# Turning keys and values with VectorE and DRAM instead of TensorE, with the transfers on GpSimd's queue

## The chip, the cores and the metric

One core of a Trainium2 chip runs the whole program. The metric is device time in microseconds; three runs of the kernel before took 852.05, 852.40 and 853.03 us, median 852.4 us.

## The reference

A sequence of 512 tokens of width 1024 goes through two layers. Each layer does an RMS norm, one wide input projection, an attention mixer, a product with SiLU of a gate, an output projection and a residual add. All data is float32.

- Layer A has three dilated head groups of 16 heads of 64 each. Group 0 is a local window, groups 1 and 2 have dilations 4 and 16. Queries and keys are RMS-normed per head; the three groups' softmaxes are merged by their denominators, so one softmax over all three groups' logits gives the same result:

```python
for g, (window, dilation) in enumerate(DILATED_PAIRS):
    q = rms_norm(qkv[:, :, g, 0], q_gain[g])
    k = rms_norm(qkv[:, :, g, 1], k_gain[g])
    v = qkv[:, :, g, 2]
    o, lse = dilated_group_attention(q, k, v, ...)
alpha = jax.nn.softmax(jnp.stack(lses), axis=0)
y = jnp.sum(alpha[..., None] * jnp.stack(outs), axis=0)
y = y.reshape(b, s, BRANCH_WIDTH).astype(hn.dtype) * jax.nn.silu(gate)
return y @ w_out
```

- Layer B is a 2-D neighbourhood attention with one head group. The change does not touch it.

## The kernel before

**Tiling.** Heads are taken in eight pairs, `hc` = 0 to 7; a pair fills 128 partitions. For each pair of layer A `main_a` runs four projections: `rawk` (keys of groups 1 and 2 beside their values, 512 columns), `rawq` (queries of the three groups and keys of group 0, 512 columns), group 0's values (`v0_a`) and the gate (`gate_a`). Products are kept exact by splitting each operand into a rounded high part and a rest: `wh` is made by ScalarE (L127), `wl` by GpSimd for two splits of five and by VectorE for the others (L131), and each product is three matmuls (`mm3`). One split of 512 weight columns feeds twelve matmuls. There are four buffers each of `wh` and `wl`, and a split is made while the three before it are still to be used.

**Attention of a pair** (`attn_a`). `scores(u)` works on two of the four query tiles, `u` = 0 and 1: its logits come from `q0h`, `k0h` (group 0) and from `qt`, `k12` (groups 1 and 2). The exponentials `p` are turned by VectorE in blocks of 32x32 (`tr`, L727), then `turner.send` writes them to DRAM (`td`, L736) and four transfers read them back (`pt`, L740), which completes the transposition. `weigh` multiplies P^T with the values `v12` and `v0`; `put_y` applies the gate. Queries of pairs 0 to 5 (`moved`) take the same way through DRAM (`move_q`: `qd`, `qt`).

**Keys and group 0's values.** `k_a` turns the keys of groups 1 and 2 on TensorE: two groups of four 128x128 transposes (L210), each copied out of PSUM by VectorE with the gain `gk` (L527). `v_a` turns `vt` on TensorE with four transposes, and ScalarE copies them to `v0` (L615).

**Order.** TensorE's order is written out by hand: `run` steps through `main` (the projections) and lets `side` (attention) put its work between them, by a clock that counts TensorE's work in nanoseconds; a 512-column matmul counts 512/2.4 = 213. `later_on(delay, job)` emits a job when that clock has advanced by `delay`. The other engines' orders come from a planner, save where `keep_in_program_order` holds an instruction behind the one traced before it on its engine. Transfers of weights, `td`, `pt`, `qd`, `qt` and biases are all issued by SyncE.

Of the kernel before, what the change touches and what calls it, by code (L numbers as in the profile page):

```python
# [13 lines left out]
F32 = mybir.dt.float32  # L14
# [28 lines left out]
def tile_hybrid_encoder(  # L43
# [222 lines left out]
    def squares(v, ss, i, ns):  # L266
        sq = wk.tile([P, 512], F32, tag="sq", name="sq")[:, : ns * 64]
        if len(v.shape) == 3:
            v = v.rearrange("p (a f) r -> p a f r", f=4)
            nc.gpsimd.tensor_mul(sq.rearrange("p (f a r) -> p a f r", f=4, a=4), v, v)  # L270
        else:
# [7 lines left out]
    def head_norm(raw, ss, ns, held, delay=0):  # L279


        rs = wk.tile([P, 32], F32, tag="rs", name="rs")
        rsqrt(nc.vector if ns == 8 else nc.gpsimd, rs[:, : 4 * ns], ss[:, : 4 * ns], 4 * ns, 1.0 / DH)

        def scale():
            for i in range(4):
                by = rs[:, i * ns : (i + 1) * ns].unsqueeze(2)
                if len(raw.shape) == 4:
                    v = raw[:, :, i, :].rearrange("p (h a f) r -> p f h a r", h=2, f=4)
                    by = rs[:, i * ns : (i + 1) * ns].rearrange("p (f h) -> p f h", h=2)  # L290
                    by = by.unsqueeze(3).unsqueeze(4).to_broadcast([P, 4, 2, 2, 32])
                else:
# [34 lines left out]
    rs_n = cp.tile([P, 4], F32, name="rs_n")  # L327
    rs_trj = cp.tile([P, S], F32, name="rs_trj")
    rs_half = cp.tile([P, S], F32, name="rs_half")
# [40 lines left out]
    def scales_a():  # L370
        pa = spread()
        nc.scalar.mul(tjr(rs_half), to_tjr(pa), 0.5)
        nc.scalar.copy(trj(rs_trj), to_trj(pa))

# [49 lines left out]

    def part(n):
        return rk[:, 1024 * n : 1024 * n + 1024].rearrange("p (i c) -> p i c", i=4)

    def project_qk(n, ns, key, hc, guard, first=False, **kw):
# [3 lines left out]
        def evac(i, acc):  # L432
            if not box:
                if key == "rawq":
                    t = wk.tile([P, 4 * n], F32, tag="rawq", name=key, bufs=1)
                    box.append(
                        t.rearrange("p (c i r) -> p c i r", c=16, i=4)
                        if moved(hc)
                        else t.rearrange("p (i c) -> p i c", i=4)
                    )  # L440
                elif key == "rawk":
                    box.append(part(0))
                    st["v12", hc] = part(1 + hc % 3)
# [8 lines left out]
            elif key == "rawk":  # L452
                pieces = [(raw[:, i, :], acc[:, :256]), (st["v12", hc][:, i, :], acc[:, 256:])]
            else:
                pieces = [(raw[:, i, :], acc[:, :n])]
            for dst, src in pieces:
                if first:
                    nc.scalar.copy(dst, src)
                else:
                    nc.scalar.activation(dst, src, AF.Copy, scale=rs_n[:, i : i + 1])  # L460
            if not first:
                squares(raw[:, :, i, :] if key == "rawq" and moved(hc) else raw[:, i, : ns * 64], ss, i, ns)

# [8 lines left out]
    def normed(raw, ss, ns, key, hc):  # L472
        head_norm(raw, ss, ns, key == "raw", 9000 if key == "rawk" and 0 < hc < NHC - 1 else 0)
        if key == "rawq" and moved(hc):
            turn_q(raw)
        st[key, hc] = raw
        stamp[key, hc] = clock[0]

    def first_out():

        raw, ss = st.pop("first")
        for i in range(4):
            for t in (raw, st["v12", 0]):
                nc.scalar.activation(t[:, i, :], t[:, i, :], AF.Copy, scale=rs_n[:, i : i + 1])
            squares(raw[:, i, :], ss, i, 4)
        normed(raw, ss, 4, "rawk", 0)
# [12 lines left out]
    def v0_a(hc):  # L499
# [3 lines left out]
        vt = wk.tile([P, EXT], F32, tag="vt", name="vt", bufs=1)  # L503
        nc.vector.tensor_mul(trj(vt[:, 64:EXT]), to_trj(acc[0]), trj(rs_trj))
        nc.gpsimd.tensor_copy(vt[:, 0:64], vt[:, EXT - 64 : EXT])
        st["vt", hc] = vt
        stamp["vt", hc] = clock[0]
# [13 lines left out]
    def k_a(hc):  # L521
        yield "wait", ("rawk", hc), 12500 if hc == 0 else 22500 if hc < NHC - 1 else 10000
        k12 = wk.tile([P, 2, 512], F32, tag="k12", name="k12", bufs=1)
        raw = st.pop(("rawk", hc))
        for g in range(2):
            tp = transpose4(raw, g * P)
            nc.vector.tensor_scalar(k12[:, g, :], tp, gk[:, g + 1 : g + 2], None, op0=ALU.mult)  # L527
# [80 lines left out]
    def v_a(hc):  # L608
# [4 lines left out]
        for i in range(4):  # L613
            transpose(tp[:, i * P : (i + 1) * P], vt[:, i * P : (i + 1) * P])
        nc.scalar.copy(v0[hc % 2], tp.rearrange("p (i c) -> p i c", i=4))  # L615
        stamp["v", hc] = 0
# [99 lines left out]
    class turner:  # L716
# [11 lines left out]

        def send(self, dst, wait, pace):

# [4 lines left out]
            src = self.t[:, : 4 * run].rearrange("p (b x) -> p b x", b=4)  # L735
            tc.keep_in_program_order(nc.sync.dma_start(d.rearrange("b p x -> p b x"), src))  # L736

            def read(b):
                src = d[b].rearrange("(a k) x -> k a x", a=4)
                tc.keep_in_program_order(nc.sync.dma_start(place[32 * b : 32 * b + 32], src))  # L740
                self.left -= 1
# [4 lines left out]
    def attn_a(hc):  # L746
# [7 lines left out]
        def scores(u):  # L754
# [94 lines left out]
        if hc < NHC - 1:  # L849
            for u in range(2):  # L850
# [285 lines left out]
    def side():  # L1136
# [20 lines left out]
        for hc in range(NHC):  # L1157
            if hc < NHC - 1:
                yield from k_a(hc)
                yield from chain(q_a(hc), v_a(hc))  # L1160
                if moved(hc):
                    yield from st.pop(("land", hc))
                yield from attn_a(hc)
                if hc == 1:
# [113 lines left out]
```

## Time and profile before

| | |
|---|---|
| median of 3 runs | 852.4 us |
| the profiled execution's own time | 854.65 us |
| its span, first to last instruction | 852.7 us |
| TensorE matmul busy | 843.6 us, 99% |
| VectorE / ScalarE / GpSimd busy | 520.2 / 431.3 / 307.1 us |
| moved by DMA | 141.23 MB |

The profile names engines PE (matmul), PEld (weight load), DVE (VectorE), ACT (ScalarE), POOL (GpSimd) and SP (SyncE). A "q" behind a name is the engine's queue, where DMAs are issued. A timeline row gives start and duration in us, the engine, the line, what is written and read, and in brackets the engine's idle time before it with what ended it. A group row gives busy time in us and the mean of one in ns. Layer A takes roughly the first 550 us, layer B the rest.

### The profile page before, as it was taken

To read this page: it belongs to the slowest core of one execution; us is meant where nothing else is said; L and a number is where in the kernel's file an instruction comes from. 1 tells how busy PE (TensorE), PEld (TensorE's weight loads), DVE (VectorE), ACT (ScalarE), POOL (GpSimd) and SP (SyncE) were. 2 spreads that over 40 slices of the span, in tenths; PEclk is the share of its full clock that TensorE was granted. 3 is DMA by queue.
4 is the path that set the end of the run, shared out by engine and by line. 5 is a ranking of instruction groups with operands and counts; after the bars stand their busy time and mean duration, and the time that the engine had idled before them with its cause. 6 is when DMAs were issued, how large, how long until landed. Compare 5 with 4: busy or idle time off the path is not lost.

```text
span 852.7 us, 15400 instructions
## 1 busy us (share of the span) xinstructions
PE 843.6 (99%) x5547; PEld 702.7 (82%) x5547; DVE 520.2 (61%) x1335; ACT 431.3 (51%) x924; POOL 307.1 (36%) x493
## 2 busy tenths in 40 slices
PE   8999999999999999999999999999999999999998
PEld 6788878788788788788788787789998898889786
DVE  6445684674675675675675745447567656766642
ACT  7433653653652652652653554355366655665531
POOL 2252541542542542542531341121344335542411
PEclk9999999999999999999999999999999999999999
DMA  7346277477478378378375562174245654555223
GB/s 250 111 130 208 87 226 219 153 222 227 137 230 241 105 239 240 98 238 238 96 247 153 147 190 78 60 244 142 82 142 150 168 162 149 170 163 160 99 98 126
DMA packets 65372, 141.23 MB, mean 166 GB/s; under 512 B 5904, under 2 KB 23248, under 8 KB 65296
## 3 DMA queue, kind: packets, MB, share of 16 engines
q1 hardware_dynamic: 65008, 140.24, 53.7%
q8 instruction: 44, 0.72, 0.4%
q14 instruction: 32, 0.26, 0.1%
q10 hardware_dynamic: 288, 0.01, 0.0%
HBM read 109.11 MB, written 31.12 MB: 164 GB/s over the span
## 4 chain that ended last, share of the span: by engine, by line
PE 87%; ACT 4%; DMA 4%; DVE 3%; issue 1%; POOL 1%; SPq 0%; ACTq 0%; POOLq 0%; DVEq 0%
PE acc L206 74%; PE log L206 5%; PE o L206 5%; PE tp L210 3%; DMA qd<-rawq 1%; ACT p L655 1%; ACT p L814 1%; DMA rp<-in_rpb 1%; ACT p L1067 1%; DMA qt<-qd 1%; POOL sq L270 1%; ACT wh L127 1%; DMA hg<-in_head_gain 0%; DVE wl L131 0%; DMA eb<-lb_d 0%
## 5 line engine op out<-in xcount | busy, mean ns | idle before, releaser
L127 ACT CAST wh<-wraw 128x512 fp32r<-128x512 f32 (+1 forms) x276 | 162.0, 588 | 291.4 <-PE acc L206 251.0
L206 PE MATMUL acc<-wh,hn_h 128*128 128x512 f32 (+1 forms) x768 | 294.2, 383 | 1.7 <-ACT wh L127 0.9
L206 PE MATMUL acc<-wh,hn_l 128*128 128x512 f32 (+1 forms) x768 | 286.3, 373 | 0.0
L206 PE MATMUL acc<-wl,hn_h 128*128 128x512 f32 (+1 forms) x768 | 285.8, 372 | 0.4 <-DVE wl L131 0.4
L131 POOL TENSOR_TENSOR wl<-wraw,wh 128x512 fp32r<-128x512 f32 (+1 forms) x110 | 137.0, 1245 | 359.4 <-ACT wh L127 320.0
L131 DVE TENSOR_TENSOR wl<-wraw,wh 128x512 fp32r<-128x512 f32 (+1 forms) x166 | 111.1, 670 | 135.8 <-ACT wh L127 131.5
L206 PEld LDWEIGHTS acc<-wh,hn_h 128*128 128x128 f32 x768 | 144.6, 188 | 29.3 <-issue 4.9
L206 PEld LDWEIGHTS acc<-wh,hn_l 128*128 128x128 f32 x768 | 144.4, 188 | 20.8
L206 PEld LDWEIGHTS acc<-wl,hn_h 128*128 128x128 f32 x768 | 144.8, 189 | 19.8 <-DVE wl L131 0.9
L206 PE MATMUL acc<-hn_h,wh 128*128 128x512 f32 x192 | 77.0, 401 | 0.9 <-ACT rawq L460 0.6
L206 PE MATMUL acc<-hn_h,wl 128*128 128x512 f32 x192 | 74.9, 390 | 0.0
L206 PE MATMUL acc<-hn_l,wh 128*128 128x512 f32 x192 | 74.8, 390 | 0.0
L655 ACT ACTIVATE p<-p,mn 128x512 f32<-128x512 f32 (+3 forms) x128 | 69.3, 586 | 0.0
L814 ACT ACTIVATE p<-p,mn 128x512 f32<-128x512 f32 (+1 forms) x64 | 44.8, 701 | 45.0 <-DVE mn L803 44.1
L273 DVE TENSOR_REDUCE ss<-sq 128x4 f32<-128x256 f32 (+1 forms) x96 | 48.4, 504 | 30.7 <-POOL sq L272 19.7
L727 DVE STREAM_TRANSPOSE tr<-p 128x512 f32<-128x512 f32 (+1 forms) x80 | 53.7, 682 | 9.9 <-ACT p L655 9.5
L272 POOL TENSOR_TENSOR sq<-rawk 128x256 f32<-128x256 f32 x64 | 40.5, 639 | 52.7 <-ACT rawk L460 44.9
L206 PE MATMUL acc<-y_h,wh 128*128 128x512 f32 x128 | 52.1, 407 | 0.0
L206 PE MATMUL acc<-y_h,wl 128*128 128x512 f32 x128 | 50.0, 391 | 0.0
L206 PE MATMUL acc<-y_l,wh 128*128 128x512 f32 x128 | 49.9, 390 | 0.0
L206 PEld LDWEIGHTS acc<-hn_h,wh 128*128 128x128 f32 x192 | 36.1, 188 | 10.8 <-ACT rawk L460 2.1
L206 PEld LDWEIGHTS acc<-hn_h,wl 128*128 128x128 f32 x192 | 36.0, 188 | 7.7
(138 smaller groups left out, 1087.0 us busy)
## 6 DMA issues: line engine op xcount, KB each, us to landing
wraw<-in_w SPq DMA_DIRECT2D x95, 512.0 KB
wraw<-in_w SPq DMA_DIRECT2D x38, 384.0 KB
td<-tr SPq DMA_DIRECT2D x14, 1024.0 KB
pt<-td SPq DMA_DIRECT2D x56, 256.0 KB
qd<-rawq SPq DMA_DIRECT2D x6, 1024.0 KB
qt<-qd SPq DMA_DIRECT2D x24, 256.0 KB
td<-tr SPq DMA_DIRECT2D x6, 896.0 KB
pt<-td SPq DMA_DIRECT2D x24, 224.0 KB
```

The lines of the kernel that those rows point to most:

```text
L127: nc.scalar.copy(h, raw)
L131: eng.tensor_sub(l, raw, h.bitcast(F32))
L206: nc.tensor.matmul(o, l, r, **kw)
L210: nc.tensor.transpose(o, i, ident)
L270: nc.gpsimd.tensor_mul(sq.rearrange("p (f a r) -> p a f r", f=4, a=4), v, v)
L272: nc.gpsimd.tensor_mul(sq, v, v)
L273: nc.vector.tensor_reduce(ss[:, i * ns : (i + 1) * ns], sq.rearrange("p (a b) -> p a b", b=64), axis=AX.X, op=ALU.add)
L655: nc.scalar.activation(pr, pr, AF.Copy, scale=mn[:, 3:4])
L727: nc.vector.transpose(dst, src[:, :n].rearrange("p (i b k) -> p i b k", b=4, k=32))
L814: nc.scalar.activation(row, row, AF.Exp, bias=mn[:, 1:2], scale=-1.0, accum_out=mn[:, 2:3])
L1067: nc.scalar.activation(pr[:, o : o + n], pr[:, o : o + n], AF.Exp, bias=mn[:, 0:1], scale=-1.0, accum_out=mn[:, 2:3])
```

## The change

- The keys of groups 1 and 2 of pairs 0 to 6 (`moved_k`) are written by the evacuation in a layout `rk_a` in which VectorE turns 32x32 blocks in place (two instructions a pair). `move_k` writes them to DRAM (`kd`) in one transfer and reads them back in four; ScalarE then applies the gain, with two instructions a pair.
- Group 0's values of pairs 0 to 5 are turned by VectorE into a free strip of the same buffer and ride with the next pair's keys; GpSimd copies them to `v0` with a factor of 2, because `vt` is now scaled with `rs_half`, and the tile `rs_trj` is gone.
- `k12` has another layout, so that the score matmuls read their moving operand in four runs of 32.
- All transfers of `kd`, and layer A's `td` and `pt` of pairs 0 to 6, are issued by GpSimd. The reads of P^T come 16000 clock units after the write with 900 between them, instead of 8500 and 1200.
- `k_a` stays for pair 7 alone, `v_a` for pairs 6 and 7.

```diff
+            if len(raw.shape) == 5:
+                for g in range(2):
+                    tc.keep_in_program_order(nc.vector.transpose(raw[:, :, g, :, :], raw[:, :, g, :, :]))
...
+    moved_k = lambda hc: hc < NHC - 1
...
+    rk_a = rk[:, :1536].rearrange("p (a y) -> p a y", a=4)
...
+        if key == "rawk" and moved_k(hc):
+            move_k(hc, 17500 if hc else 4000)
...
-        nc.vector.tensor_mul(trj(vt[:, 64:EXT]), to_trj(acc[0]), trj(rs_trj))
+        nc.vector.tensor_mul(
+            in_trj(vt[:, 64:EXT], "t r j"), in_trj(acc[0], "j t r"), in_trj(rs_half, "t j r")
+        )
         nc.gpsimd.tensor_copy(vt[:, 0:64], vt[:, EXT - 64 : EXT])
+        if moved(hc):
+            src = vt[:, :S].rearrange("p (i b x) -> p i b x", i=4, b=4)
+            dst = rk_a[:, :, 256:].rearrange("p b (i x) -> p i b x", i=4)
+            tc.keep_in_program_order(nc.vector.transpose(dst, src))
+            stamp["v", hc] = 0
+            return
...
+    def move_k(hc, delay):
+        n = 384 if hc else 256
+        d = dr.tile([4, P, 384], F32, name="kd", tag="kd", bufs=2)
+        box = []
+        def write():
+            tc.keep_in_program_order(nc.gpsimd.dma_start(d.rearrange("a p y -> p a y")[:, :, :n], rk_a[:, :, :n]))
+            stamp["k12", hc] = 0
+        def read(a):
+            if not box:
+                box.append(wk.tile([P, 4, 384], F32, tag="k12", name="k12", bufs=1))
+            dst = box[0][32 * a : 32 * a + 32, :, :n]
+            src = d[a].rearrange("(b k) y -> k b y", b=4)[:, :, :n]
+            tc.keep_in_program_order(nc.gpsimd.dma_start(dst, src))
+        def landed():
+            kv = box[0]
+            for g in range(2):
+                k = kv[:, :, P * g : P * g + P]
+                tc.keep_in_program_order(nc.scalar.activation(k, k, AF.Copy, scale=gk[:, g + 1 : g + 2]))
+            if hc:
+                src = kv[:, :, 256:].rearrange("p b (i x) -> p b i x", i=4)
+                dst = v0[(hc - 1) % 2].rearrange("p i (b x) -> p b i x", b=4)
+                tc.keep_in_program_order(nc.gpsimd.tensor_scalar(dst, src, 2.0, None, op0=ALU.mult))
+            st["k12", hc] = kv, st.pop(("v12", hc))
+        later_on(delay, write)
+        for n_, a in enumerate((0, 2, 1, 3)):
+            later_on(delay + 16500, partial(read, a))
+        later_on(delay + 29500, landed)
...
-        def send(self, dst, wait, pace):
+        def send(self, dst, wait, pace, by=nc.sync):
...
-                                k12[hs, g, P * j : P * j + P],
+                                sb(k12[hs], P * g + 32 * j, [[384, 4], [1, 32]]),
...
-                send = partial(turned.send, pq[:, 2048 * u : 2048 * u + 2048], 8500, 1200)
+                send = partial(turned.send, pq[:, 2048 * u : 2048 * u + 2048], 16000, 900, nc.gpsimd)
...
-                yield from k_a(hc)
-                yield from chain(q_a(hc), v_a(hc))
+                yield from q_a(hc)
                 if moved(hc):
                     yield from st.pop(("land", hc))
+                else:
+                    yield from v_a(hc)
```

More of the change, by code (lines that the diff above doesn't have):

```diff
@@ L270, in squares @@
             nc.gpsimd.tensor_mul(sq.rearrange("p (f a r) -> p a f r", f=4, a=4), v, v)
+        elif len(v.shape) == 4:
+            nc.gpsimd.tensor_mul(sq.rearrange("p (g a x) -> p a g x", g=2, a=4), v, v)
         else:
@@ L460, in evac @@
                     nc.scalar.activation(dst, src, AF.Copy, scale=rs_n[:, i : i + 1])
-            if not first:
-                squares(raw[:, :, i, :] if key == "rawq" and moved(hc) else raw[:, i, : ns * 64], ss, i, ns)
+            if first:
+                return
+            if key == "rawk" and moved_k(hc):
+                v = raw[:, :, :, i, :]
+            elif key == "rawq" and moved(hc):
+                v = raw[:, :, i, :]
+            else:
+                v = raw[:, i, : ns * 64]
+            squares(v, ss, i, ns)
         tile_of = lambda hn: lambda k, i: hn[:, k, P * i : P * (i + 1)]
@@ L475, in normed @@
             turn_q(raw)
+        if key == "rawk" and moved_k(hc):
+            move_k(hc, 17500 if hc else 4000)
         st[key, hc] = raw
@@ L521, in k_a @@
     def k_a(hc):
-        yield "wait", ("rawk", hc), 12500 if hc == 0 else 22500 if hc < NHC - 1 else 10000
-        k12 = wk.tile([P, 2, 512], F32, tag="k12", name="k12", bufs=1)
+        yield "wait", ("rawk", hc), 10000
+        k12 = wk.tile([P, 4, 384], F32, tag="k12", name="k12", bufs=1)
         raw = st.pop(("rawk", hc))
```

40 lines of the change are left out of this document (26 added, 14 removed).

## The prediction

> **What bounds the kernel now.** I read the profile's first page first, then TensorE's waits. From the page, two of the first lines:
>
> ```profile
> span 852.7 us, 15400 instructions
> PE 843.6 (99%) x5547; PEld 702.7 (82%) x5547; DVE 520.2 (61%) x1335; ACT 431.3 (51%) x924; POOL 307.1 (36%) x493
> ```
>
> Only 9.1 us of the span have no matmul. In the view of waits TensorE has six rows, each shorter in total than the first, under 5 us together:
>
> ```profile
> PE acc L206 <- ACT rawq L460: 1.4, 2, 0.8
> ```
>
> So TensorE's instructions themselves are the bound: what is taken off it comes off the time, if nothing new makes it wait. The busy total cannot price an instruction, as matmuls overlap; spacing in the timeline can. Here are TensorE's rows around one group of key transposes and one group of value transposes:
>
> ```profile
> 56.77 0.39 PE L206 MATMUL acc<-hn_h,wl 128*128 128x512 f32 x1
> 57.01 0.60 PE L210 MATMUL tp<-ident,rawk 128*128 128x128 f32 x4
> ...
> 58.60 0.39 PE L206 MATMUL acc<-hn_h,wl 128*128 128x512 f32 x1
> ...
> 60.66 0.39 PE L206 MATMUL acc<-hn_h,wh 128*128 128x512 f32 x1
> ...
> 61.79 0.39 PE L206 MATMUL acc<-hn_h,wl 128*128 128x512 f32 x1
> ...
> 74.71 0.39 PE L206 MATMUL acc<-wh,hn_l 128*128 128x512 f32 x1
> ...
> 76.54 0.39 PE L206 MATMUL acc<-wh,hn_l 128*128 128x512 f32 x1
> ```
>
> Undisturbed, five steps of the projection take 61.79 - 60.66 = 1.13 us, 0.227 each. From 56.77 to 58.60 are six projection steps and one group of four transposes: 1.83 us, of which the six steps are 1.36. **A group of four costs TensorE 0.47 us** (the 0.60 of its row overlaps its neighbours). The value group from 74.71 to 76.54, again six steps, costs 0.47 too.
>
> **What the change takes off TensorE.** In the view of the tile `tp`:
>
> ```profile
> L210 PE MATMUL tp<-ident,rawk x128: 270/272/273, 57.0 to 803.9; 128*128 128x128 f32 x128
> L210 PE MATMUL tp<-ident,vt x32: 270/272/274, 74.9 to 549.4; 128*128 128x128 f32 x32
> ```
>
> Of the 128 with `rawk`, 64 are layer A's keys, 8 a pair (layer B's raw tiles share the buffer's name). Seven pairs lose 2 groups each and six pairs a value group: 14 + 6 = 20 groups, 80 transposes. 20 x 0.47 = **9.4 us**. What else could be gained is bounded by TensorE's own waits, under 5 us, of which none is on the parts removed.
>
> The score matmuls stay in number, but read `k12` in runs of 32 instead of 128 (so does pair 7). The nearest rows are P^T's products, which already read runs of 32, and the scores as they are:
>
> ```profile
> L206 PE MATMUL o<-pt,rawk 128*64 128x128 f32 x320 | 22.4, 278 | 0.9 <-DMA eb<-lb_d 0.9
> L206 PE MATMUL log<-k,qt 64*32 64x128 f32 x1024 | 18.9, 274 | 0.0
> ```
>
> 278 against 274 ns for 128 columns: I cost the layout at nothing; the high end is a rival below.
>
> **What it adds to VectorE, ScalarE and GpSimd.** Groups by form:
>
> ```profile
> L535 DVE STREAM_TRANSPOSE rawq<-rawq 128x512 f32<-128x512 f32 x24 | 16.0, 688 | 0.0
> L527 DVE TENSOR_SCALAR k<-tp,gk 128x512 f32<-128x512 f32 x16 | 11.5, 720 | 0.8 <-PE tp L210 0.8
> L615 ACT COPY v<-tp 128x512 f32<-128x512 f32 x8 | 4.7, 585 | 5.9 <-PE tp L210 5.9
> ```
>
> VectorE: 20 transposes x 0.69 less 14 evacuations x 0.72 = +3.7 us over layer A. ScalarE: 14 gain passes x 0.59 (the copy's price) less 6 copies and the one of `rs_trj` = +4.1 us. GpSimd: six copies of `v0`, at most 1.32 each (its `wl` of that size, quoted below, has two inputs) = +7.9 us. None is on TensorE's path while these engines keep ahead of it. One period of a pair shows how much room there is; columns are the stretch, its length, and busy time of PE, PEld, DVE, ACT, POOL:
>
> ```profile
> 286.60:350.70 64.10, 64.10 (x454) 52.13 (x452) 41.18 (x100) 32.25 (x63) 24.62 (x36) 1.00 0.64 192
> ```
>
> VectorE and ScalarE gain under 1 us in each 64.1, beside 22.9 and 31.9 us idle; the granted clock is 1.00.
>
> **The moved transfers, the real risk.** GpSimd gets 15 transfers a pair: `td` twice, `pt` eight times, `kd` once, and its four reads. No row before shows GpSimd issuing one. On SyncE's queue such a transfer occupies the queue for (minimum/median/maximum ns)
>
> ```profile
> L740 SPq DMA_DIRECT2D pt<-td x80: 312/423/1553, 110.9 to 778.9; - x80
> L736 SPq DMA_DIRECT2D td<-tr x20: 377/382/1623, 105.1 to 765.0; - x20
> ```
>
> Call GpSimd's price of one c. The bounds by these rows are 0.31 and 1.62 us; I take the medians, 0.4, the same instruction. Behind a transfer GpSimd holds the next `wl`, and TensorE waits for that. How late may a `wl` be?
>
> ```profile
> L127 ACT CAST wh<-wraw 128x512 fp32r<-128x512 f32 x196 | 121.1, 619 | 217.0 <-PE acc L206 180.5 <-DMA wraw<-in_w 21.2 <-issue 8.8
> L131 POOL TENSOR_TENSOR wl<-wraw,wh 128x512 fp32r<-128x512 f32 x81 | 106.7, 1317 | 287.7 <-ACT wh L127 263.5 <-issue 9.3 <-DVE mn L1057 5.8
> ```
>
> The cast waits for TensorE (180.5 us) to free one of four buffers; three splits of 12 x 0.227 = 2.72 us are then still ahead. So 8.16 - 0.62 - 1.32 = **6.2 us of slack**. The tightest place is the end of `rawq` in each period, in GpSimd's and SyncE's timelines:
>
> ```profile
> 309.45 3.43 POOL L270 TENSOR_TENSOR sq<-rawq 128x512 f32<-128x512 f32 x3 [0.79 <-ACT rawq L460]
> 312.84 1.29 POOL L131 TENSOR_TENSOR wl<-wraw,wh 128x512 fp32r<-128x512 f32 x1
> 314.10 1.48 POOL L270 TENSOR_TENSOR sq<-rawq 128x512 f32<-128x512 f32 x1
> 316.96 0.63 POOL L505 COPY vt<-vt 128x64 f32<-128x64 f32 x1 [1.38 <-DVE vt L504]
> 319.37 1.28 POOL L131 TENSOR_TENSOR wl<-wraw,wh 128x512 fp32r<-128x512 f32 x1 [1.78 <-ACT wh L127]
> ```
>
> ```profile
> 296.12 0.38 SPq L736 DMA_DIRECT2D td<-tr  x1
> ...
> 310.47 0.38 SPq L736 DMA_DIRECT2D td<-tr  x1
> ```
>
> The program's clock runs 0.227/0.213 = 1.064 slower on the chip. The first P^T write stays at 296.1, so its four reads move to 296.1 + 17.0 = 313.1 to 316.0; the second write stays at 310.5. `rawk` of this period ends near 281.4 (the chain of waits has its `weigh` behind it at 281.75), so the keys' reads, 34000 later, come at 317.6. Nine transfers thus fall between 310.5 and the `wl` of 319.37, where GpSimd has 8.9 us less 2.4 + 1.3 + 1.5 + 0.6 = 3.1 us free. That `wl` is late by 9c - 3.1, and TensorE waits once 9c - 3.1 > 6.2: **from c = 1.03 us on**. At 0.4 the lateness is 0.5 us and costs nothing. On the same queue stand the squares, for whose sums VectorE waits, and the copy of `vt`, for which the new transpose of the values waits, with VectorE's own `wl` behind it; they have fewer transfers ahead of them (three and five), so they decide later than the `wl`.
>
> Do the new waits hold? From the chain of waits, one write of 1024 KB and four reads of 256 KB through DRAM:
>
> ```profile
> 201.33 10.40 DMA qd<-rawq
> ...
> 213.78 5.63 DMA qt<-qd
> 281.75 3.62 PE o L206 x48
> ```
>
> P^T's reads now come 17.0 us after their write and the keys' 17.6 us after theirs, against 10.4, so GpSimd need not stand waiting; the keys' reads have 13.8 us to land before ScalarE's gain passes (47000 units behind `rawk`, at 331.4), against 5.6. SyncE loses these waits altogether.
>
> Here one page speaks against the change: the Trainium skill, "SBUF — State Buffer", section "SBUF: two separate sides", says that a transfer issued by GpSimd has its descriptors written by GpSimd's own cores, which cannot write while VectorE runs an instruction that takes both ports, and gives about 0.62 us alone and 3.1 beside such an instruction. By the first figure as c, an estimate, the sum is mine; by the second, 18.6 us would be lost in every period. No run here shows it yet, and VectorE's work in that stretch has few plain copies, the case the page names.
>
> **The sum.** 852.7 - 9.4 = 843.3 us of span, to which the profiled execution adds 854.65 - 852.7 = 1.95. That execution was 2.25 us above the median of the runs; against the median, 852.4 - 9.4 = **843.0 us**, my forecast.
>
> **Rivals.**
>
> *GpSimd's issuing holds the `wl` (ends slower).* A GpSimd instruction of one shape does not always take the same time here:
>
> ```profile
> L505 POOL COPY vt<-vt x8: 237/631/731, 63.0 to 513.6; 128x64 f32<-128x64 f32 x8
> ```
>
> So GpSimd is held by something, up to threefold. A c of 0.42 x 731/237 = 1.3 us loses 9 x 1.3 - 9.3 = 2.4 us in each of the six periods (pairs 1 to 6) that have both the keys' and P^T's transfers: 14.4 us, **857 us**. It decides from 1.03, and gain and loss balance at 6(9c - 9.3) = 9.4, c = 1.21. At c = 1.12 it takes back half the gain: 847.7. At SyncE's maximum of 1.62 it would be 843 + 31.7 = 875. Against it: the medians are far below 1.03. The page named above would be the cause of such a hold; by its second figure the loss would be the larger one given there.
>
> *The strided keys slow the scores.* If the 1024 matmuls with the keys, 18.9 us busy, took twice as long, this would be 843 + 18.9 = 862 us. The row of 278 ns speaks against it.
>
> *The transfers disturb the weights.* The change moves 2 x 0.79 MB more a period on top of 192 GB/s x 64.1 us = 12.3 MB, and two queues now share the engines. ScalarE already waited 21.2 us for weights (the row above) without TensorE stopping. If each period of six gave back 1.3 us, 851 us, no change.
>
> **How the numbers follow.** The forecast has 0.64 (its own range 841 to 847: 2 us of TensorE's present waits gone too, and up to 4 us of small new ones). GpSimd's issuing has 0.24: 0.08 for c between 1.03 and 1.21, most of it still faster, 0.16 beyond. The strided keys have 0.04, the disturbed weights 0.08, mostly no change. A measurement of this kernel tells about 0.2%, 1.7 us. Faster: 0.64 + 0.06 = 0.70; same: 0.02 + 0.07 = 0.09; slower: 0.16 + 0.04 + 0.01 = 0.21. The range goes from 841 to 857, the rival at 1.3 us; it leaves out the worse half of that rival and the strided keys, under 2 in 10.
>
> **What would show it.** Right: 80 fewer `tp` matmuls, TensorE's waits still under some 8 us, the spacing of the `log` matmuls unchanged, GpSimd's transfers well under 1 us. Wrong: TensorE waiting for `wl` of GpSimd at the end of `rawq`, in each period; VectorE waiting for `vt`; scores stretched beyond 1.2 us for 64.

## The result, and the profile after

The changed kernel is slower. Four runs took 861.42, 862.03, 865.15 and 865.85 us, against a median of 852.22 us for the kernel before on the same chip; the ratio is 1.0125 (95% interval 1.0111 to 1.0138). Two further runs, of 875.27 us (granted clock 0.982) and of 2122.08 us, fall in the slow state and are left out of it. The forecast was 843.0 us, the range 841 to 857. The profiled execution of after is the one of 861.42 us, the fastest of the four, and the profiled one of before (854.65 us) lay 2.4 us above its median; so the two profiles show 6.9 us of the 11.4 us between the medians.

From the page of after (span, engines, DMA queues, and the engines' shares of the chain that ended last):

```profile
span 859.6 us, 15330 instructions
PE 842.8 (98%) x5467; PEld 698.8 (81%) x5467; DVE 530.2 (62%) x1341; ACT 434.7 (51%) x931; POOL 374.6 (44%) x604
...
q1 hardware_dynamic: 49552, 110.87, 43.0%
...
q0 software_dynamic: 11312, 39.85, 16.0%
...
PE 80%; DMA 7%; DVE 6%; ACT 3%; issue 1%; SPq 1%; POOL 0%; ACTq 0%; DVEq 0%; POOLq 0%
```

TensorE has 80 matmuls fewer (5547 to 5467), yet its busy time is almost the same and the span is 6.9 us longer. `q0` is GpSimd's DMA queue, new in this kernel. TensorE's waits in after (us in total, times, longest):

```profile
PE log L206 <- ACT q0h L695: 3.4, 5, 1.1
PE acc L206 <- ACT rawq L479: 1.9, 2, 1.1
PE log L206 <- DVE q0l L699: 1.5, 5, 0.3
PE tp L210 <- DVE rawq L301: 1.2, 1, 1.2
```

The new rows that recur are the first and the third (the fourth is a single wait): at the first scores of pairs 1 to 5 TensorE waits for the split queries and keys of group 0 (`q0h`, `q0l`). ScalarE makes these splits behind the arrival of `qt`, the queries' way through DRAM. That way is later by steps. From TensorE's side each stall starts a second loss; two stretches of after (length, busy time and instructions of PE, PEld, DVE, ACT, POOL, then the granted clock, the DMA share, GB/s):

```profile
286.60:350.70 64.10, 63.02 (x426) 51.21 (x426) 43.26 (x101) 32.39 (x63) 32.81 (x46) 0.97 0.71 208
290.40:293.80 3.40, 3.40 (x71) 2.69 (x72) 1.57 (x9) 1.39 (x2) 1.85 (x2) 0.50 0.02 5
```

After the stall at 288 us the granted clock is 0.50 for 3.4 us; the same happens once more at 161 us. Each dip loses 3.4 x 0.5 = 1.7 us. Reading the spacing of TensorE's instructions in the timeline, the stalls at the five first scores come to about 9.5 us, other new stalls to about 3, the dips to 3.4: 9.4 us saved, some 16 lost, which is the +6.9 of the span.

**Where the queries are late.** VectorE's timelines from the third sum of squares to the end of the queries' turn, before and then after:

```profile
312.91 0.69 DVE L273 TENSOR_REDUCE ss<-sq 128x8 f32<-128x512 f32 x1 [0.31 <-POOL sq L270]
...
320.96 2.50 DVE L295 TENSOR_TENSOR rawq<-rawq,rs 128x512 f32<-128x512 f32 x4
...
326.79 1.29 DVE L535 STREAM_TRANSPOSE rawq<-rawq 128x512 f32<-128x512 f32 x2
```

The same rows of after, with those between that are new there:

```profile
316.68 0.69 DVE L275 TENSOR_REDUCE ss<-sq 128x8 f32<-128x512 f32 x1 [0.31 <-POOL sq L270]
...
325.57 0.69 DVE L131 TENSOR_TENSOR wl<-wraw,wh 128x512 fp32r<-128x512 f32 x1 [1.13 <-ACT wh L127]
326.18 1.35 DVE L115 SCALAR_TENSOR_TENSOR na<-na,nv 128x32 f32<-128x32 f32 x1
327.46 0.68 DVE L523 TENSOR_TENSOR gt<-gt,rs_half 128x512 f32<-128x512 f32 x1
...
328.27 3.60 DVE L301 TENSOR_TENSOR rawq<-rawq,rs 128x512 f32<-128x512 f32 x4
...
332.46 2.48 DVE L608 STREAM_TRANSPOSE rawq<-rawq 128x512 f32<-128x512 f32 x4
```

From the sum to the end of the turn it was 328.08 - 312.91 = 15.2 us and is 334.94 - 316.68 = 18.3: a `wl` that waits for ScalarE and a step of the gate (`gt`) now stand ahead of the queries' scaling, and the scaling itself takes 3.6 us instead of 2.5. GpSimd's timeline of after shows a part of the cause:

```profile
317.84 0.79 POOL L809 DMA_DIRECT2D td<-tr  x1
318.63 0.56 POOL L813 DMA_DIRECT2D pt<-td  x1
319.20 1.05 POOL L270 TENSOR_TENSOR sq<-rawq 128x512 f32<-128x512 f32 x1
...
329.39 1.33 POOL L131 TENSOR_TENSOR wl<-wraw,wh 128x512 fp32r<-128x512 f32 x1 [1.91 <-ACT wh L127]
```

Two transfers, 1.35 us, now stand ahead of the fourth square of the queries. And a scaling is not slower as such: three of the four take 0.69 us, and the one that runs beside the `wl` of 329.39 takes 1.78. Of the 32 scalings in layer A, seven take about 1.78 us in after, and each of the seven starts while a `wl` of GpSimd is running; the other 25 take 0.68 to 0.69 us. Before, two are long.

Then the transfers, in SyncE's timelines before and after:

```profile
329.79 0.43 SPq L578 DMA_DIRECT2D qd<-rawq  x1
...
336.39 1.75 SPq L584 DMA_DIRECT2D qt<-qd  x4
```

and in after:

```profile
335.97 0.43 SPq L651 DMA_DIRECT2D qd<-rawq  x1
...
346.50 1.75 SPq L657 DMA_DIRECT2D qt<-qd  x4
```

Between the queries' write and their reads lay 6.6 us, and now 10.5. Not every pair is like this one, pair 4: in pairs 1 and 2 the time did not grow (9.1 and 10.5 us before, 7.3 and 9.9 in after), in pairs 3 to 5 it grew by 2.5 to 4.1. The slack shows at the other end. Before, the split `q0h` of this pair starts at 346.25 us, 4.8 us ahead of the first scores (351.00); in after it starts at 354.41, and the scores follow it directly, at 355.18. Why the write takes longer is seen in the queues of after from 336 to 340 us (packets, MB, share of the 16 DMA engines' time):

```profile
q0 software_dynamic: 272, 0.89, 98.9%
q1 hardware_dynamic: 16, 0.04, 4.4%
```

The queries' write was given to SyncE's queue at 335.97 and gets almost nothing for these four microseconds, while the reads on GpSimd's queue are being served. At the end of this way ScalarE, which the page before shows with no lack of time, stands still (timeline of after):

```profile
338.83 1.34 ACT L593 ACTIVATE k<-k,gk 128x512 f32<-128x512 f32 x2 [4.91 <-DMA k<-kd]
...
353.40 1.10 ACT L676 CAST k0h<-qt 128x512 fp32r<-128x512 f32 x1 [5.06 <-DMA qt<-qd]
```

### The profile page after: what moved, and what is told of

The parts are those of the page before. It is cut to its first block, busy times and chain, and to the rows that moved or that the text cites. A ratio compares the mean times of both kernels' runs of the same rounds, so it can differ in the third digit from the quotient of the medians.

```text
span 859.6 us, 15330 instructions
## 1 busy us (share of the span) xinstructions
PE 842.8 (98%) x5467; PEld 698.8 (81%) x5467; DVE 530.2 (62%) x1341; ACT 434.7 (51%) x931; POOL 374.6 (44%) x604
## 4 chain that ended last, share of the span: by engine, by line
PE 80%; DMA 7%; DVE 6%; ACT 3%; issue 1%; SPq 1%; POOL 0%; ACTq 0%; DVEq 0%; POOLq 0%
PE acc L206 70%; PE log L206 5%; DMA qt<-qd 3%; PE o L206 3%; DMA qd<-rawq 2%; PE tp L210 2%; DMA k<-kd 1%; DVE rawq L301 1%; ACT k0h L676 1%; SPq L657 1%; ACT p L728 1%; DVE k0l L679 1%; DVE wl L131 1%; ACT p L1140 1%; DVE rawq L608 0%
## 5 line engine op out<-in xcount | busy, mean ns | idle before, releaser
L131 POOL TENSOR_TENSOR wl<-wraw,wh 128x512 fp32r<-128x512 f32 (+1 forms) x110 | 139.9, 1272 | 281.8 <-ACT wh L127 252.5
L131 DVE TENSOR_TENSOR wl<-wraw,wh 128x512 fp32r<-128x512 f32 (+1 forms) x166 | 113.6, 686 | 125.1 <-ACT wh L127 120.8
L800 DVE STREAM_TRANSPOSE tr<-p 128x512 f32<-128x512 f32 (+1 forms) x80 | 54.1, 686 | 13.8 <-ACT p L728 11.7
L206 PEld LDWEIGHTS acc<-hn_h,wh 128*128 128x128 f32 x192 | 36.1, 188 | 11.4 <-ACT rawk L479 2.1
L206 PEld LDWEIGHTS acc<-hn_l,wh 128*128 128x128 f32 x192 | 36.1, 188 | 6.8
```

What stands on the lines that cost most here:

```text
L131: eng.tensor_sub(l, raw, h.bitcast(F32))
L206: nc.tensor.matmul(o, l, r, **kw)
L800: nc.vector.transpose(dst, src[:, :n].rearrange("p (i b k) -> p i b k", b=4, k=32))
```

## The experiments

The theory from these readings, called D: TensorE's saving is real, and the keys' and values' new way through DRAM makes the queries late, by its bytes and by being issued from GpSimd. The rivals: the price lies in GpSimd's issuing alone (G), or in one badly placed read that can be moved. Ratios are to the kernel before, timed on the same chip. Times of `later_on` are units of the program's clock.

**Queries that do not wait for their way (q_free).** Pairs 1 to 5 read the previous pair's queries, ahead of their own pair's write; the right queries of these pairs are left out.

```diff
-            src = d[a].rearrange("(t k) x -> k t x", t=4)
+            src = d_read[a].rearrange("(t k) x -> k t x", t=4)   # tile of the pair before
...
-            later_on(5500, partial(read, a))
+            later_on(0 if hc else 5500, partial(read, a))
+        if hc:
+            later_on(600, write)                                 # behind the reads
```

> The changed kernel, but pairs 1 to 5 read their queries from the DRAM tile that the pair before wrote (so their queries are the wrong pair's; that part of the computation is left out), and the reads are issued before this pair's write and don't wait for it. Theory Q: the loss is TensorE waiting for queries that come late through DRAM (in the changed kernel's trace about 9 us at the first scores of pairs 1 to 5, and clock dips behind it). Then those waits go and only small stalls near 68, 115 and 458 to 478 us stay, about 4 us: 846 to 849 us. Rival G: GpSimd's 15 transfers a pair hold the weight splits, which this leaves alone: 860 to 864 us, no change to the changed kernel. Rival S: the strided keys slow the scores, also left alone: 860 us or more.

855.17 us, ratio 1.0009 (0.9990 to 1.0028): 10 us better than after, so this wait is the larger part of the loss, but not all. TensorE's waits in this run have no row for `log` any more; the next in line shows instead:

```profile
PE acc L206 <- ACT rawk L479: 2.1, 3, 1.2
```

ScalarE evacuates `rawk` late. What stands directly ahead of the evacuation, in ScalarE's order, is a `wh` that waits for its weights: in the pair of 340 us for 4.00 us, and these weights were issued at 330.35 us and landed at 340.48. The gain passes wait for the keys 5.08 us too, but earlier, and ScalarE has caught up in between. So here it is the weights that the new transfers make late. The run lies between the ranges of the two theories and inside neither.

**Who issues: four combinations.** `pt_pool_only` is the kernel before with P^T's transfers on GpSimd, at after's times. `pt_sync` and `k_sync` are after with P^T's or the keys' transfers back on SyncE; `all_sync` has both back. Where P^T goes back, its reads go back to the times of before too.

```diff
 pt_sync, all_sync:
-  ... 16000, 900, nc.gpsimd)
+  ... 8500, 1200)
 k_sync, all_sync:
-  nc.gpsimd.dma_start(...kd...)
+  nc.sync.dma_start(...kd...)
```

> The kernel before with P^T's transfers alone on GpSimd at 16000 and 900; keys and values stay on TensorE. Theory D: the second P^T reads now overlap the queries' write and go ahead of it, but 0.79 MB less stands in the stretch; the queries come 2 to 3 us later than before, about at their need: 852 to 857 us. If moving P^T to GpSimd costs nothing: 852.4 us; if GpSimd's issuing is itself the loss: 860 us or more.

> The changed kernel with P^T's transfers back on SyncE at 8500 and 1200; keys and values stay on GpSimd. Theory Q with its cause, that GpSimd's queue is served ahead of SyncE's, so that the queries' write waits for the second P^T reads: these reads now stand in SyncE's own order and end before the queries' write; the queries land 4 us or more earlier, TensorE's waits for them go: 845 to 850 us. If instead VectorE and GpSimd bring the queries late (their turn ends 3 us later than before, still so here in part): 854 to 860 us.

> The changed kernel with the keys' and values' transfers on SyncE and P^T's on GpSimd: the fourth corner beside the changed kernel, P^T on SyncE, and all on SyncE. Theory D, engines full and GpSimd's queue served first: the keys' reads stand in SyncE's own queue behind P^T's and just ahead of the queries' write, so the queries are as late as in the changed kernel: 858 to 866 us. If the keys on GpSimd's queue were the loss alone: like all on SyncE, 855 to 858 us.

> The changed kernel with every transfer on SyncE (P^T at 8500 and 1200, keys and values at the changed kernel's delays). Tells the turning through DRAM from GpSimd's queue. Theory Q with GpSimd's queue as its cause: TensorE's saving of 9.4 us is kept but for small stalls: 844 to 850 us. If the 1.57 MB more in each period are the cause, whoever issues them: 856 us or more.

| P^T issued by | keys and values issued by | ratio (95%) |
|---|---|---|
| GpSimd | not moved (`pt_pool_only`) | 1.0009 (0.9997 to 1.0022) |
| GpSimd | GpSimd (after) | 1.0125 (1.0111 to 1.0138) |
| SyncE | GpSimd (`pt_sync`) | 1.0121 (1.0074 to 1.0168) |
| GpSimd | SyncE (`k_sync`) | 1.0084 (1.0055 to 1.0113) |
| SyncE | SyncE (`all_sync`) | 1.0045 (1.0030 to 1.0059) |

Moving P^T alone costs the kernel before nothing that can be measured. With the keys' way added, all on SyncE is the best of the four, still slower than before: GpSimd's issuing, with the later reads of P^T that go with it, is worth 0.8%, and something else takes back the whole saving. `pt_sync` (866.88 us) missed both of its ranges, the theory's by far; `k_sync` (859.87) fell into the range of theory D, `all_sync` (856.83) into that of the bytes as the cause, whoever issues them, and `pt_pool_only` (854.40) into a range that left both open. A part of `pt_sync` is the clock: its profiled execution, of 867.73 us, has a granted clock of 0.50 in four stretches, at 72, 229, 362 and 427 us, 20 us in all, so it loses 10 us by dips, and after 3.4.

In `all_sync` the queries are late too, by fewer but longer stalls, and the clock falls again; its wait for them, from TensorE's waits:

```profile
PE log L206 <- ACT q0h L695: 2.9, 2, 2.6
```

The stretch of `all_sync` behind the longest of these stalls, with the columns of the stretches above:

```profile
222.70:229.50 6.80, 6.67 (x83) 5.19 (x82) 4.62 (x22) 3.40 (x8) 3.23 (x2) 0.54 0.01 2
```

Here the clock stays near half for twice 3.4 us.

**The keys' reads at another time.** `k_early`: reads 9000 behind their write instead of 16500. `k_earlier`: also scaled at 7000 and written at 13500. `all_sync_early`: `all_sync` with the reads at 8000. `keys_read_pool`: `all_sync_early` with these reads alone issued by GpSimd.

```diff
-            later_on(delay + 16500, partial(read, a))
+            later_on(delay + 9000, partial(read, a))      # k_early; 8000 if hc in all_sync_early, keys_read_pool
```

> The changed kernel with the keys' four reads 9000 clock units behind their write instead of 16500; all on GpSimd. They fall into a stretch where the DMA engines are nearly idle, and the second P^T reads end some 3.5 us earlier, so the queries' write starts earlier. Theory Q with GpSimd's queue as its cause: 848 to 853 us. If VectorE and GpSimd's instructions set the lateness, the four issues now stand ahead of the queries' squares on GpSimd, 2.2 us: 864 to 868 us.

> The changed kernel, all on GpSimd, with the keys scaled at 7000, written at 13500 and read 9000 behind that, so that the reads fall ahead of the queries' squares and into the idle stretch; the gain passes stay where they were. Theory D: the second P^T reads end some 3 us earlier, the queries' write on SyncE's queue is served earlier by as much, and TensorE's waits shrink from about 2 us a period to under 1: 849 to 855 us. If GpSimd's queue going first is not what holds the queries: 860 to 865 us.

> All transfers on SyncE as in the run before (856.8 us), and the keys' four reads of pairs 1 to 6 issued 8000 clock units behind their write instead of 16500, into a stretch where the DMA engines are nearly idle. Theory D: the engines are full from the end of the queries' projection to the next pair's scores, the keys' reads stand there ahead of the queries' write, and TensorE waits for queries. Then taking 0.79 MB (some 3 us) out of that stretch brings the queries 3 us earlier; the two waits of the trace before (219 and 352 us, 5.4 us with their pieces) and the clock dips behind them (5.1 us) go: 844 to 848 us, faster than both kernels. Rival: the queries are late because VectorE and GpSimd reach the turn late, whatever the transfers: 855 to 858 us.

> all_sync_early with the reads of keys and values alone issued by GpSimd, all writes and P^T on SyncE. If the queries are late there because SyncE's order puts the keys' read waits ahead of the second td write and the queries' write: 846 to 850 us, against 852.0 for all_sync_early. If GpSimd's queue, served ahead of SyncE's, is what delays the queries' transfers: 854 to 862 us.

`k_early` took 872.13 us, 1.0211 (1.0157 to 1.0264), `k_earlier` 890.25 us, 1.0421 (1.0392 to 1.0450): both missed, and far on the wrong side. The trace of `k_earlier` shows one way in which the earlier transfers stand ahead of others. In `k_earlier` the keys' write goes first, then the write of P^T's blocks (GpSimd's timeline below), and VectorE, which has one buffer `tr` for these blocks, waits for it; the sums of squares and the queries come behind:

```profile
316.09 0.82 POOL L579 DMA_DIRECT2D kd<-rawk  x1 [2.92 <-DVE rawk L306]
316.92 0.76 POOL L809 DMA_DIRECT2D td<-tr  x1
```

and on VectorE, in the same run:

```profile
326.64 2.49 DVE L800 STREAM_TRANSPOSE tr<-p 128x512 f32<-128x512 f32 x4 [4.88 <-DMA td<-tr]
```

`all_sync_early` took 851.99 us, 0.9987 (0.9972 to 1.0001): level with before, 4 us short of what was expected. `keys_read_pool` took 869.46 us, 1.0177 (1.0145 to 1.0210), the opposite of the first expectation and worse than the second: with only the four reads a pair on GpSimd, SyncE waits much longer for its own writes. SyncE's waits for `td` in `keys_read_pool`:

```profile
SPq L813 <- DMA td<-tr: 80.3, 11, 16.0
```

and in `all_sync_early`:

```profile
SPq L813 <- DMA td<-tr: 28.8, 12, 6.1
```

Behind these waits on SyncE stand the weights; TensorE there waits for their splits (4.3 us for `wh`, 2.6 us for GpSimd's `wl`).

**How many bytes.** `k_third` sends only 128 of the 384 columns through DRAM, in as many transfers; the rest of these keys and values is left out (zeros stand in its place). `both_free` is `q_free` with the keys and values of pairs 2 to 6 also read from the previous pair's tile, 4500 after `delay`; the right ones are left out.

```diff
 k_third:
-        n = 384 if hc else 256
+        n = 128
...
 both_free (beside q_free's edit):
-            src = d[a].rearrange("(b k) y -> k b y", b=4)[:, :, :n]
+            src = d_read[a].rearrange("(b k) y -> k b y", b=4)[:, :, :n]   # tile of the pair before
...
-            later_on(delay + 16500, partial(read, a))
+            later_on(delay + (4500 if d_read is not d else 16500), partial(read, a))
```

> The kernel after with only 128 of the columns of the dilated keys and values sent through DRAM (into a tile zeroed once); the rest of these keys and values is left out. The number of instructions and the waits stay, the bytes of this way fall to a third: about 1.05 MB less in a period. Theory D with bytes as the cause (the DMA engines are nearly full in the stretch before the next scores): 848 to 854 us, DMA share of that stretch back near 0.85, queries' scale start some 2 us earlier. Rival G (order of work and issues on GpSimd and VectorE set the lateness): 858 to 865 us.

> q_free (queries of pairs 1 to 5 read from the previous pair's DRAM tile) with the dilated keys and values of pairs 2 to 6 also read from the previous pair's DRAM tile, some 4500 after the loads, so that neither waits on a write of its own pair; all transfers, issues and sums stay. The right queries and keys are left out for those pairs. Theory D (the saving of 9.4 us is real, and is lost only because queries and keys come late through DRAM): 843 to 848 us, no wait of TensorE at the first scores and none of ScalarE on the keys' landing over 1 us. Rival G (the price lies in GpSimd's and VectorE's added work, which still stands here): 853 to 860 us.

`k_third` took 855.3 us, 1.0021 (1.0006 to 1.0037). With the instructions and the order unchanged, two thirds of the bytes are worth some 9 us of the loss. Its waits have no row for `q0h`; the first is

```profile
PE tp L210 <- DVE rawq L301: 1.9, 3, 1.3
```

One part of the expectation failed: the DMA share of the stretch before the next scores did not fall. That stretch of 35 us in the kernel before:

```profile
310.00:345.00 35.00, 35.00 (x158) 28.96 (x157) 19.53 (x37) 13.55 (x27) 13.62 (x14) 1.00 0.85 248
```

in after:

```profile
314.00:349.00 35.00, 35.00 (x158) 28.75 (x158) 22.34 (x40) 14.12 (x28) 22.81 (x29) 1.00 0.93 255
```

and in `k_third`:

```profile
311.00:346.00 35.00, 35.00 (x187) 28.56 (x186) 19.51 (x37) 13.21 (x25) 21.16 (x38) 1.00 0.94 258
```

The stretch is as full in `k_third` as in after, though the bytes of the new way fell to a third. What fills the room instead no run separates; that it is weights for the next period is likely and not shown. What counts is what stands ahead of the queries, not the share.

`both_free` took 864.11 us, 1.0119 (1.0086 to 1.0152), and decides nothing: the four reads now stand between GpSimd's squares at the end of `rawq`, and in pair 6 TensorE waits 5.4 us for VectorE's `rawq` behind them. It tests its own new order. Its waits at the first scores are gone, as in `q_free`.

**Values taken out of the new way.** Four kernels let TensorE turn group 0's values for every pair again, so that only keys go through DRAM (256 columns instead of 384), which gives back 6 x 0.47 = 2.8 us of the saving. They differ in the issuer and in the time of the keys' reads. A fifth, `novalues_bytes`, sends 384 columns all the same, with zeros that nobody reads.

```diff
-        n = 384 if hc else 256
+        n = 256                      # novalues_bytes: 384 if hc else 256
...
-        if moved(hc):                # VectorE's turn of vt
+        if False:
...
-            if hc:                   # GpSimd's copy to v0
+            if False:
...
+                yield from v_a(hc)   # for every pair but the last two, which have it already
```

> all_sync_early (every transfer on SyncE, keys read 8000 after their write) with the values of layer A turned by TensorE again for every pair, so that only keys go the new way. It gives back 6 x 0.47 = 2.8 us of the saving, and takes away a third of the added bytes and the values' copies. Theory D (lateness by bytes and by work ahead of the queries): 846 to 850 us, stalls at the first scores under 0.6 us. If the remaining stalls do not come from the values' part: 854 to 857 us.

> The kernel after with the values of layer A turned by TensorE again; keys still go through DRAM, keys' and P^T's transfers still issued by GpSimd. If the values' part (a third of the bytes, and VectorE's and GpSimd's work on them) makes the difference: 849 to 853 us, as all_sync_early_novalues. If GpSimd's queue, served ahead of SyncE's, is a cause by itself: 855 to 862 us.

> all_sync_early_novalues with the keys' reads at 16500 after the write, as in the kernel after, every transfer on SyncE. If the early reads are worth something by themselves (all_sync 1.0045 to all_sync_early 0.9987 with values): 852 to 855 us. If values alone made the queries late: 848 to 850 us.

> all_sync_early_novalues with P^T's transfers issued by GpSimd, as in the kernel after. P^T's move alone made no difference to the kernel before (1.0009). Theory: no difference here either, 848 to 851 us. If GpSimd's queue holds the keys' and queries' transfers of SyncE up: 853 to 858 us.

> all_sync_early_novalues with the values' columns sent through DRAM all the same (zeros, not read), so the bytes of all_sync_early stay and the values' work on VectorE and GpSimd is gone. If the bytes make the queries late: 852 to 855 us (the 852.0 of all_sync_early, and 2.8 us for the 24 transposes given back). If the work on VectorE and GpSimd does: 848 to 850 us.

| kernel | issued by; keys' reads | time, us | ratio (95%) |
|---|---|---|---|
| `after_novalues` | all GpSimd; 16500 | 859.66 | 1.0060 (1.0038 to 1.0082) |
| `novalues_pt_pool` | P^T GpSimd, keys SyncE; 8000 | 853.72 | 1.0005 (0.9991 to 1.0019) |
| `all_sync_novalues` | all SyncE; 16500 | 850.07 | 0.9956 (0.9938 to 0.9974) |
| `all_sync_early_novalues` | all SyncE; 8000 | 849.39 | 0.9952 (0.9937 to 0.9968) |
| `novalues_bytes` | all SyncE; 8000; 384 columns | 855.96 | 1.0020 (1.0003 to 1.0037) |

Four things follow.

1. The saving on TensorE is real. In `all_sync_early_novalues` 14 groups are gone, 14 x 0.47 = 6.6 us; its span is 847.3 us, 5.4 below before (by the ratio, 4.1), and its waits are back to those of a kernel that nothing new holds up:

```profile
PE acc L206 <- ACT rawq L479: 1.8, 2, 1.1
...
PE acc L206 <- ACT wh L127: 0.5, 1, 0.5
```

2. The values cost through their bytes. Zeros in their place, with no work on VectorE or GpSimd, make 0.9952 to 1.0020, 0.0068 or 5.8 us. The values in earnest (`all_sync_early`, 0.9987) save 2.8 us of TensorE's time on top of that, 0.0033: just the difference of the two.

3. GpSimd as issuer, with P^T's reads at their later times, costs by itself: 1.0060 against 0.9956 without values, 8.9 us, and 1.0125 against 1.0045 with them, 6.8 us. VectorE shows a part of it. From the third sum of squares to the end of the queries' turn, `after_novalues` takes 330.59 - 312.64 = 18.0 us, as after does, and `all_sync_novalues` 325.61 - 310.88 = 14.7, as before does, so this delay does not come from the values' turn on VectorE. The collisions of scalings with GpSimd's `wl` go with the issuer: nine long scalings in `after_novalues`, one in `all_sync_novalues`. VectorE's timeline of `after_novalues`:

```profile
312.64 0.69 DVE L275 TENSOR_REDUCE ss<-sq 128x8 f32<-128x512 f32 x1 [0.31 <-POOL sq L270]
...
323.93 3.58 DVE L301 TENSOR_TENSOR rawq<-rawq,rs 128x512 f32<-128x512 f32 x4
...
328.70 1.89 DVE L608 STREAM_TRANSPOSE rawq<-rawq 128x512 f32<-128x512 f32 x3
```

and of `all_sync_novalues`:

```profile
310.88 0.69 DVE L275 TENSOR_REDUCE ss<-sq 128x8 f32<-128x512 f32 x1 [0.31 <-POOL sq L270]
...
319.51 2.50 DVE L301 TENSOR_TENSOR rawq<-rawq,rs 128x512 f32<-128x512 f32 x4
...
324.32 1.29 DVE L608 STREAM_TRANSPOSE rawq<-rawq 128x512 f32<-128x512 f32 x2
```

   The way of the same pair's queries in five kernels, in us, from the timelines of ScalarE, VectorE, SyncE and TensorE, shows where the slack goes:

| kernel | end of `rawq`'s evacuation to write | write to first read | first read to split `q0h` | split to first scores |
|---|---|---|---|---|
| before | 18.4 | 6.6 | 9.9 | 4.8 |
| `pt_pool_only` | 18.0 | 10.1 | 7.2 | 4.2 |
| `all_sync_novalues` | 17.9 | 9.6 | 7.8 | 3.9 |
| `all_sync` | 19.0 | 11.8 | 7.7 | 0.8 |
| after | 20.8 | 10.5 | 7.9 | 0.8 |

   At 0.8 us, about the length of the split itself, TensorE waits. Ten us between write and read alone make no stall. In `all_sync` the transfers take the slack, in after the late write and the transfers together. That SyncE issues everything does not shorten the time from write to read.

4. Two expectations fell. P^T on GpSimd, free for the kernel before, costs 0.0053 or 4.5 us once the keys go through DRAM (`novalues_pt_pool`). And the early reads are worth nothing without the values (0.9952 and 0.9956, inside each other's intervals), though they were worth 0.0058 with them.

`all_sync_early_novalues` is faster than both kernels; `all_sync_novalues` cannot be told from it.

## Why the prediction was wrong, step by step

- *The saving, 9.4 us off TensorE*: right. 80 matmuls are gone, and where nothing else is in the way the saving of 14 groups, 6.6 us, shows up in the span all but 1.2 us.
- *Strided keys at nothing*: right. The score row has 274 ns in `after_novalues`, as before. After's own row has 286, with dips of the clock among its scores:

```profile
L206 PE MATMUL log<-k,qt 64*32 64x128 f32 x1024 | 20.0, 286 | 0.0
```

- *GpSimd's price of one transfer, c = 0.4*: mis-sized, without consequence where it was thought to matter. After's groups on GpSimd:

```profile
L813 POOL DMA_DIRECT2D pt<-td x56 | 31.0, 557 | 6.7 <-DMA pt<-td 5.4 <-issue 1.3
L587 POOL DMA_DIRECT2D k<-kd x28 | 15.3, 552 | 7.4 <-DMA td<-tr 7.4
L809 POOL DMA_DIRECT2D td<-tr x14 | 11.3, 807 | 1.4 <-DVE tr L800 1.4
L579 POOL DMA_DIRECT2D kd<-rawk x7 | 5.6, 800 | 7.6 <-DVE rawk L306 7.6
```

  Reads 0.55, writes 0.80, all under the 1.03 from which a `wl` would have been late; after has no wait for GpSimd's `wl`. The rival that named this hold gave 857 us, nearer to the result than the forecast, by a mechanism that did not occur in after. But the step also said of the squares and of VectorE's work behind them that "they decide later than the `wl`", and that did not hold: the queries' scaling starts 13.1 us behind the end of their evacuation in the pair shown, and 9.5 before, and the queries' write is 2.4 us later by it. The Trainium skill, "SBUF — State Buffer", section "SBUF: two separate sides", gives 0.62 us for a transfer of GpSimd alone and 3.1 beside VectorE's two-port work: the time for which a read holds GpSimd lies near the first figure, and no transfer of GpSimd here held it over 0.937 us.
- *Do the new waits hold?* Here it failed. The step asked whether P^T's and the keys' reads would have their data when issued, and whether the keys would land in time. It did not ask the same of the queries, whose write and reads stay on SyncE, through the same DMA engines in the same stretch. It called the loss of waits on SyncE a gain ("SyncE loses these waits altogether") without costing what the bytes moved to another queue do to the transfers left on it. In the pair shown the queries' write to reads went from 6.6 to 10.5 us, and the write itself came 2.4 us later behind their evacuation; together they used up the 4.8 us by which the split was early, and TensorE waited at the first scores of pairs 1 to 5. `k_third` shows the part of the bytes: with two thirds of them gone, 9 us of the loss are gone.
- *The keys' 13.8 us to land*: also failed. The reads were issued at 323.1 to 326.2 us in the pair shown, not at 317.6, and landed so late that ScalarE stood 4.9 us at its gain passes. These passes are in ScalarE's order ahead of the evacuations and splits that TensorE needs, which the prediction did not cost; no wait of TensorE in after is put down to them, so what it costs is not shown.
- *VectorE +3.7, ScalarE +4.1 us*: ScalarE gained 3.4, VectorE 10.0. The turn of the values needs `vt` in another layout, and more of the queries' scalings run beside a `wl` of GpSimd:

```profile
L533 DVE TENSOR_TENSOR vt<-acc,rs_half 128x512 f32<-128x512 f32 x8 | 8.8, 1105 | 6.2 <-PE acc L206 6.1
L301 DVE TENSOR_TENSOR rawq<-rawq,rs 128x512 f32<-128x512 f32 x32 | 27.6, 925 | 0.2
```

  Before, these were 5.5 us (682 ns each) and 22.2 us (755). GpSimd's six copies of `v0`, put at 1.32 us each at most, take 1.50. "None is on TensorE's path" was judged by the idle time of a whole period; but the queries' sums, scaling and turn are a chain, and what is put into it delays the write.
- *The rival of disturbed weights*, 1.3 us a period, used the mean of the whole period, 192 GB/s and a DMA share of 0.64. In the 35 us before the next scores it was 248 GB/s and 0.85 already. It had the right cause, added bytes on shared engines, and the wrong victim: the queries come first, and the weights show in `q_free`, where nothing waits for queries (2.1 us of TensorE's waits), and in `keys_read_pool`.
- No step priced a stall beyond its own length; the trace of before, which has no stall at the scores, has a granted clock of 1.00 in the period shown, and so no dip to price.

What stays open: how the 7 to 9 us of GpSimd's issuing divide between GpSimd's time ahead of the squares, the scalings that collide with its `wl`, the order of VectorE's instructions, the queue that goes ahead of SyncE's, and the dips of the clock, which no run separated.

## What to carry to other kernels

When work is moved from the engine that bounds a kernel to DMA, follow every transfer that stays, not only the new ones, through the stretch where the data is due: look for the chain with the next deadline (here the queries) and count what now stands ahead of it on each queue and engine. Judge room by that stretch and not by the mean of a period. Move the part that saves most for its bytes: the keys alone, with all transfers left on SyncE, made the kernel 0.5% faster, and the values on top gave most of that back at the best times found for the reads (0.9987), and more than all of it at those of after (1.0045).

## What the runs showed of the hardware

- **GpSimd's DMA queue can keep SyncE's waiting.** In after, with both queues holding work from 336 to 340 us, `q0` had 98.9% of the engines' time and `q1` 4.4% (rows above). It is not so at all times: from 333 to 336 us, as P^T's last reads are issued 1 us apart (the last at 333.52), `q0` had 36.8% and `q1` 68.4%. The Trainium skill, "DMA: Bandwidth & Descriptors", section "Queues, rings and completion order", says that each engine takes turns between the queues that have work, packet by packet. The rows of 336 to 340 us do not agree with equal turns. With only the keys' reads on GpSimd, SyncE's waits for its own `td` writes went from 28.8 to 80.3 us.
- **A short stall can cost TensorE twice.** Stalls of some 1.5 to 4 us in all at the scores were followed by 3.4 or 6.8 us at a granted clock of 0.5 in after (at 161 and 290 us) and in `all_sync` (at 222 and 355 us); not every stall was (in after, that at 355 us, of some 2.4 us, was not). In `all_sync` the dips lost (6.8 + 3.4) / 2 = 5.1 us, nearly as much as the stalls themselves, some 5.4.
- **A transfer issued by GpSimd occupies it** for 0.55 us (256 KB and 192 KB reads) to 0.80 us (writes of 768 KB and 1 MB), against 0.42 and 0.38 us on SyncE for P^T's; the 84 reads, of both sizes, lie between 551 and 592 ns.
- **VectorE and GpSimd held each other up in products of two tiles.** The scaling of the queries on VectorE (L301, 128x512) takes 0.68 to 0.69 us, and 1.76 to 1.81 us in the seven of 32 cases of after in which a `wl` of GpSimd had started 0.05 to 0.48 us before it. In the five cases in which the `wl` started while a scaling was running, that scaling kept its 0.68 to 0.69 us, and the `wl` took 1.33 to 1.72 us, against 1.27 to 1.30 for most.
